# Moving the start addresses of matmul operands in SBUF, and the adaLN sums by one job turn

## The chip, the cores and the metric

The kernel runs on one core of a Trainium2 chip. The metric is the device time of one execution in microseconds (us): the median of three runs is 3477.94 (3477.12 to 3479.91). PE is the matmul engine, PEld its weight loads, DVE, ACT and POOL the three element-wise engines, SP the queue that issues most DMAs.

## The reference

Two transformer-like blocks of two layers each over a sequence of 512 tokens of width 1024, all in float32. What is computed, cut down:

```
first_block, per layer:   ada = silu(c) @ w_ada + b_ada          # adaLN: six vectors of 1024
                          u   = h * (1 + sc1) + sh1
                          y   = mixer(u)    # mLSTM (4 heads), dilated attention (24 heads), gates, w_a, w_b, w_out
                          h   = layer_norm(ALPHA * h + g1 * y)
                          u   = h * (1 + sc2) + sh2
                          h   = layer_norm(ALPHA * h + g2 * ((silu(u @ w1) * (u @ w3)) @ w2))
second_block, per layer:  adaLN, RMS norm, then RG-LRU + stick-breaking attention (layer 0)
                          or windowed attention (layer 1), then a gated FFN with a small convolution
```

Nearly all arithmetic is in products of a 1024- or 2816-wide activation with a weight matrix.

## The kernel before

**Split products.** Activations lie transposed, 128 channels by 512 tokens, in *slots* of 2048 bytes per partition; 60 slots are handed out first in, first out (`get`, `put`). A product needs float32 accuracy, so each operand is split into a high and a low part (`hl`, `split`), and each 128 by 128 weight block costs three matmuls, called a triple here: high x high, low activation x high weight, high activation x low weight. Matmuls of the split type are one pass; each is preceded by the load of its stationary operand (PEld), which runs while the matmul ahead streams.

**Weights.** All 4176 blocks come as one stream: SP loads 16 blocks (1 MB) into `wt`; per *unit* of 8 blocks ACT casts the high part `wh` and DVE subtracts for the low part `wl` (`block`, L589 and L592). Five `wh` and five `wl` tiles rotate, so ACT and DVE run up to 40 blocks ahead of PE.

**Three kinds of split product.** `proj` (L604 to L606; its twins are `begin`, L667 to L669, and the first product, L1367 to L1369) moves a slot's 512 columns over a weight block that stands still: *full* products. `proj_halves` (L649, L652, L653) does the same for 256 columns at a time, at the ends of the layers, where a norm waits: *half* products. `proj_tokens` (L625, L628, L629) lets 256 columns of weights move over 128 columns of a slot: *moving-weight* products. In the mLSTM heads, L961 to L963 multiply two slots in the same three-step way, 512 columns each.

**Where things lie.** The tiles' sizes, in the order in which the pools take them, give every start. Before, each slot begins 448 bytes past a multiple of 512, and each `wh` and `wl` tile 384 bytes past one; a block within a unit is 512 bytes, and half a slot 1024, so all blocks and halves share these. Counted modulo 512, the moving start minus the stationary start is then 64 in full and half products, 448 in moving-weight products, and 0 where slots meet slots (L961 to L963).

**adaLN.** `ada` is a background job. One call of `background()` (a job turn) stands in each pass of the mixer's gate loops and of the FFN loops. A group of 4 x 512 outputs takes four turns, each with four 512 KB loads of `wada` (two buffers) and eight DVE steps into one slot (L776, L778); in the fourth turn, behind the last DVE step, four matmuls sum over partitions (L786), and a last turn transposes and writes columns (L794 on).

**Order.** Queues are in order, and a scheduler places instructions on each engine by what it reckons to be ready; the order below is its outcome. In `attention_pair` each of four query tiles takes, for two heads x, a score slot `p` and a transposed slot `pt`; `bts` are the bias tiles, loaded on POOL's queue (L1115).

Of the kernel before, what the change touches and what calls it, by code (L numbers as in the profile page):

```python
# [10 lines left out]
F32 = mybir.dt.float32  # L11
F32R = mybir.dt.float32r
# [4 lines left out]
P = 128  # L17
# [9 lines left out]
NBLK = 4176  # L27
CHUNK = 16
NCHUNK = NBLK // CHUNK
NSLOT = 60  # L30
NTAIL = 3
NT8 = 5
TT = ['ev_w_out_2']
UNIT = 8
# [161 lines left out]
class Slot:  # L196
# [4 lines left out]
    def __init__(self, i, ap, rounded):  # L201
        self.i = i
        self.r = ap if rounded else None
        self.f = ap.bitcast(F32) if rounded else ap
# [319 lines left out]
class Model:  # L524
    def __init__(self, ctx, tc, ins, out, dbg=None, stop=None):
        self.tc, self.nc, self.ins, self.out, self.dbg_out, self.stop = tc, tc.nc, ins, out, dbg, stop
        self.plan = []
        pool = lambda name, bufs, **kw: ctx.enter_context(tc.tile_pool(name=name, bufs=bufs, **kw))
        self.cp = pool("cp", 1)
        self.wtp = pool("wtp", 2)  # L530
        self.whp = pool("whp", 5)
        self.adp = pool("adp", 2)
        self.drp = pool("drp", 2, space=bass.MemoryType.DRAM)
        self.sm = pool("sm", 4)
        self.pacc = pool("pacc", 3, space=PSUM)
        self.pss = pool("pss", 2, space=PSUM)
        self.pst = pool("pst", 1, space=PSUM)
        self.pso = pool("pso", 2, space=PSUM)
        self.slots = pool("slots", 1)
        self.freeq = deque(range(NSLOT))  # L540
        self.peak = NSLOT
        self.late = []
        self.flip = 0
        self.ready = {}
        self.jobs = deque()
        self.later = []


    def get(self, rounded=False):
# [28 lines left out]
    def block(self, name, l, k, c):  # L578
        nc = self.nc
        n = len(self.plan)  # L580
        self.plan.append((name, l, k, c))
        if n % CHUNK == 0:
            self.wt = self.wtp.tile([P, CHUNK * P], F32, name="wt")
            nc.sync.dma_start(out=self.wt, in_=self.ins["ws"][n // CHUNK].rearrange("p a b -> p (a b)"))
        if n % UNIT == 0:
            self.wh = self.whp.tile([P, UNIT * P], F32R, name="wh")
            self.wl = self.whp.tile([P, UNIT * P], F32R, name="wl")
            src = self.wt[:, (n % CHUNK) * P:(n % CHUNK + UNIT) * P]
            copy = nc.scalar.copy(self.wh, src)  # L589
            if n == 0:  # L590
                self.behind(copy, self.last_rsqrt)
            nc.vector.tensor_tensor(out=self.wl, in0=src, in1=self.wh, op=ALU.subtract)  # L592
        s = slice((n % UNIT) * P, (n % UNIT + 1) * P)
        return self.wh[:, s], self.wl[:, s]
# [14 lines left out]
    def proj_tokens(self, name, l, c, xs):  # L609

        nc = self.nc
        ws = []
        for k in range(len(xs)):
            n = len(self.plan) % UNIT * P
            self.block(name, l, k, c)
            self.block(name, l, k, c + P)
            ws.append((self.wh[:, n:n + 2 * P], self.wl[:, n:n + 2 * P]))
        accs = []
        for a in range(2):
            accs.append(self.pacc.tile([P, T], F32, name="acc"))  # L620
            last = None
            for b in range(2):
                acc, jj = accs[a][:, 256 * b:256 * b + 256], slice((2 * a + b) * P, (2 * a + b + 1) * P)
                for k, (wh, wl) in enumerate(ws):
                    m = nc.tensor.matmul(acc, xs[k].h.r[:, jj], wh, start=k == 0, stop=False)  # L625
                    if k == 0:
                        self.behind(m, last)
                    nc.tensor.matmul(acc, xs[k].l.r[:, jj], wh, start=False, stop=False)  # L628
                    last = nc.tensor.matmul(acc, xs[k].h.r[:, jj], wl, start=False, stop=k == len(xs) - 1)  # L629
        return accs  # L630

    def proj_halves(self, specs, xs, k0=0, by_input=False):


        nc = self.nc
        n = len(xs)
        accs = [self.pacc.tile([P, T], F32, name="acc") if a < 3 else self.pso.tile([P, T], F32, name="o")
                for a in range(len(specs))]
        order = [(a, k) for a in range(len(specs)) for k in range(n)]
        if by_input:  # L640
            order.sort(key=lambda ak: ak[1])
        blks = {}
        last = [None] * len(specs)
        for hs in HALVES:
            for a, k in order:
                if (a, k) not in blks:
                    blks[a, k] = self.block(*specs[a][:2], k0 + k, specs[a][2])
                (wh, wl), acc = blks[a, k], accs[a]
                m = nc.tensor.matmul(acc[:, hs], wh, xs[k].h.r[:, hs], start=k == 0, stop=False)  # L649
                if k == 0:  # L650
                    self.behind(m, last[a])
                nc.tensor.matmul(acc[:, hs], wh, xs[k].l.r[:, hs], start=False, stop=False)  # L652
                last[a] = nc.tensor.matmul(acc[:, hs], wl, xs[k].h.r[:, hs], start=False, stop=k == n - 1)  # L653
                yield hs, a, k == n - 1, acc
# [45 lines left out]
    def setup(self):  # L700
# [3 lines left out]
        n = CST["ident"]  # L704
# [13 lines left out]
        self.zero = zero.to_broadcast([P, T])  # L718
        self.mhalf = self.cp.tile([P, 4], F32, name="mhalf")
        nc.gpsimd.memset(self.mhalf, -0.5)  # L720
        self.ident_r = self.cp.tile([P, 128], F32R, name="ident_r")
        nc.vector.tensor_copy(self.ident_r, self.ident)
        self.csil = self.cp.tile([P, 16], F32, name="csil")
        c = self.vec("c1", 0, 16)
        th = self.small(16, "th_c")
        nc.scalar.activation(th, c, AF.Tanh, scale=0.5)
        nc.vector.tensor_scalar(out=th, in0=th, scalar1=0.5, scalar2=0.5, op0=ALU.mult, op1=ALU.add)
        nc.vector.tensor_mul(self.csil, th, c)
# [20 lines left out]
            for l in range(DEPTH):  # L749
                self.adac[blk, l] = self.cp.tile([P, 48], F32, name=f"ada{blk}{l}")  # L750

        self.vn = [self.cp.tile([P, 4, 258], F32R, name=f"vn{k}") for k in range(2)]
        for k in range(2):
            col = self.small(4, "vcol")
            nc.gpsimd.memset(col, (1 - k) / 16.0)
            for j in (256, 257):
                nc.vector.tensor_copy(self.vn[k][:, :, j], col)


    def ada(self, blk, l, groups):  # L760
        nc = self.nc
        w = self.ins["ada1" if blk == 0 else "ada2"][l]
        bias = f"b_ada{l}" if blk == 0 else f"ada_b{l}"
        ad = self.adac[blk, l]
        for g in groups:
            accs = []
            for n in range(4):
                acc = self.get()
                for q in range(4):
                    wt = self.adp.tile([P, 2, T], F32, name="wada")  # L770
                    nc.sync.dma_start(out=wt, in_=w[4 * g + n, q])
                    for j in range(2):
                        k = 2 * q + j
                        c = self.csil[:, 8 * blk + k:8 * blk + k + 1]
                        if k == 0:
                            nc.vector.tensor_scalar(out=acc.f, in0=wt[:, j, :], scalar1=c, scalar2=None, op0=ALU.mult)  # L776
                        else:
                            nc.vector.scalar_tensor_tensor(out=acc.f, in0=wt[:, j, :], scalar=c, in1=acc.f,  # L778
                                                           op0=ALU.mult, op1=ALU.add)
                accs.append(acc)  # L780
                if n < 3:
                    yield

            rows = self.pss.tile([P, T], F32, name="s")
            for n, acc in enumerate(accs):
# [73 lines left out]

    def load_rsqrt(self, dep):  # L860

        t = self.small(1, "arsd")
        return self.nc.scalar.activation(t, dep, AF.Abs_reciprocal_sqrt, bias=1.0, scale=0.0)


# [179 lines left out]
    def attention_pair(self, l, sp, u):  # L1045
# [62 lines left out]
        o0 = self.pso.tile([P, T], F32, name="o")  # L1108
        o12 = self.pso.tile([P, T], F32, name="o")
        self.lastmm = {}  # L1110
        ls, mx = self.small(16, "att_l"), self.small(16, "att_m")
        cols = lambda ap, x, i: ap.rearrange("p (x y i) -> p x y i", x=2, y=2)[:, x, :, i]
        bts = [self.get(), self.get()]
        for x in range(2):
# [1 line left out]
        for i in (0, 3, 1, 2):  # L1116
            ii = slice(i * P, (i + 1) * P)
            lo, hi = max(0, i * P - 64), min(T, i * P + 192)
            w, u0, at = hi - lo, lo - (i * P - 64), min(lo, T - 256)
# [9 lines left out]
            for x in range(2):  # L1129
# [17 lines left out]
                t = self.pst.tile([P, T], F32, name="t")  # L1147
# [36 lines left out]
        t = self.pst.tile([P, T], F32, name="t")  # L1184
# [5 lines left out]
        w, l0 = self.get(), self.get()  # L1190
# [641 lines left out]
```

## Time and profile before

| | |
|---|---|
| median of three runs | 3477.94 us |
| the profiled execution | 3481.36 us, of which span 3479.6 us |
| PE, PEld busy | 98%, 80% of the span |
| DVE, ACT, POOL busy | 62%, 42%, 5% |
| mean granted TensorE clock | 0.993 |

A matmul's row in the trace is longer than the step from its start to the next start, since neighbours overlap; the pace of PE is read from starts. The difference between the execution and its span, 1.8 us, lies around the span.

### The profile page before, as it was taken

What the parts mean: (1) busy time and instruction counts of PE and PEld (TensorE: products, weight loads), DVE (VectorE), ACT (ScalarE), POOL (GpSimd) and SP (SyncE); (2) the same over time, 40 slices, a digit from 0 to 9 for tenths busy, and PEclk for the clock granted to TensorE, in tenths of its full rate; (3) what the DMA queues carried; (4) which work ended last, traced back from release to release, by engine and by line L of the source; (5) the groups of instructions that cost most, each with busy time, mean ns of one, the idle gap of its engine ahead of it and who ended that gap; (6) DMA issues with size and microseconds to landing.
All of it is one profiled execution on the core that took longest, in us unless ns stands there. A gap on an engine that the chain in (4) does not pass through costs nothing.

```text
span 3479.6 us, 45264 instructions
## 1 busy us (share of the span) xinstructions
PE 3405.2 (98%) x17783; PEld 2787.9 (80%) x17783; DVE 2159.5 (62%) x4071; ACT 1450.8 (42%) x2536; POOL 183.8 (5%) x252
## 2 busy tenths in 40 slices
PE   7999999999999999999999999989999999999999
PEld 5788777778888888877788888877688888888887
DVE  5875545648663687554534856378888555875353
ACT  4543555225222454355523422237753234753231
POOL 1110010010000011001100000001000000000000
PEclk9999999999999999999999999999999999999999
DMA  5222223634552222222222555221146432122222
GB/s 218 91 75 84 75 78 105 223 121 176 205 188 97 73 91 79 80 84 73 79 97 85 200 187 194 94 71 61 37 145 232 163 114 85 50 74 97 97 97 73
DMA packets 76117, 395.72 MB, mean 114 GB/s; under 512 B 9200, under 2 KB 10480, under 8 KB 42496
## 3 DMA queue, kind: packets, MB, share of 16 engines
q1 hardware_dynamic: 69408, 377.90, 30.5%
q0 software_dynamic: 4480, 12.69, 1.2%
q8 instruction: 140, 2.29, 0.3%
q10 hardware_dynamic: 2016, 2.25, 0.2%
q14 instruction: 73, 0.60, 0.1%
HBM read 390.60 MB, written 2.20 MB: 113 GB/s over the span
## 4 chain that ended last, share of the span: by engine, by line
PE 85%; DVE 7%; ACT 2%; DMA 2%; issue 1%; POOL 0%; DVEq 0%; ACTq 0%; POOLq 0%
PE acc L604 22%; PE acc L606 21%; PE acc L605 21%; PE acc L649 2%; PE acc L652 2%; PE acc L653 2%; DMA wada<-in_ada_dram 1%; PE o L1168 1%; PE o L1583 1%; DVE wl L592 1%; PE s L1132 1%; DVE slot L778 1%; PE acc L625 1%; PE acc L629 1%; PE acc L628 1%
## 5 line engine op out<-in xcount | busy, mean ns | idle before, releaser
L604 PE MATMUL acc<-slot,wh 128*128 128x512 f32 x3461 | 1375.7, 398 | 14.0 <-DVE slot L874 9.3
L605 PE MATMUL acc<-slot,wh 128*128 128x512 f32 x3461 | 1364.0, 394 | 0.0
L606 PE MATMUL acc<-slot,wl 128*128 128x512 f32 x3461 | 1363.3, 394 | 0.0
L589 ACT CAST wh<-wt 128x1024 fp32r<-128x1024 f32 x522 | 547.2, 1049 | 1230.0 <-PE acc L605 1021.9
L592 DVE TENSOR_TENSOR wl<-wt,wh 128x1024 fp32r<-128x1024 f32 x522 | 647.7, 1242 | 526.1 <-ACT wh L589 521.3
L604 PEld LDWEIGHTS acc<-slot,wh 128*128 128x128 f32 x3461 | 652.7, 189 | 164.2 <-ACT wh L589 13.9
L606 PEld LDWEIGHTS acc<-slot,wl 128*128 128x128 f32 x3461 | 652.1, 188 | 146.6 <-issue 4.9
L605 PEld LDWEIGHTS acc<-slot,wh 128*128 128x128 f32 x3461 | 652.9, 189 | 140.8 <-issue 5.4
L778 DVE SCALAR_TENSOR_TENSOR slot<-wada,csil,slot 128x512 f32<-128x512 f32 x308 | 232.1, 754 | 63.2 <-DMA wada<-in_ada_dram 57.6
L649 PE MATMUL acc<-slot,wh 128*128 128x256 f32 x726 | 206.9, 287 | 6.2 <-ACT slot L512 5.9
L652 PE MATMUL acc<-slot,wh 128*128 128x256 f32 x726 | 205.6, 283 | 0.0
L653 PE MATMUL acc<-slot,wl 128*128 128x256 f32 x726 | 204.3, 282 | 0.1
L680 ACT CAST slot<-slot 128x512 fp32r<-128x512 f32 x204 | 125.3, 620 | 168.9 <-DVE slot L1332 47.2
L1266 DVE SCALAR_TENSOR_TENSOR slot<-acc,ada,slot 128x512 f32<-128x512 f32 (+1 forms) x109 | 70.2, 647 | 160.8 <-PE acc L606 120.8
L874 DVE SCALAR_TENSOR_TENSOR slot<-acc,vecs,slot 128x510 f32<-128x510 f32 (+2 forms) x217 | 159.9, 746 | 7.8 <-ACT slot L869 5.2
L681 DVE TENSOR_TENSOR slot<-slot,slot 128x512 fp32r<-128x512 f32 x204 | 144.4, 714 | 30.8 <-ACT slot L680 21.3
L649 PEld LDWEIGHTS acc<-slot,wh 128*128 128x128 f32 x726 | 136.8, 189 | 13.4 <-ACT slot L512 6.5
L652 PEld LDWEIGHTS acc<-slot,wh 128*128 128x128 f32 x726 | 137.3, 189 | 2.5 <-issue 1.2
L653 PEld LDWEIGHTS acc<-slot,wl 128*128 128x128 f32 x726 | 137.4, 189 | 0.7 <-DVE wl L592 0.3
L625 PE MATMUL acc<-wh,slot 128*128 128x256 f32 x288 | 81.5, 283 | 0.0
L628 PE MATMUL acc<-wh,slot 128*128 128x256 f32 x288 | 81.4, 283 | 0.0
L629 PE MATMUL acc<-wl,slot 128*128 128x256 f32 x288 | 80.9, 281 | 0.0
(391 smaller groups left out, 3939.6 us busy)
## 6 DMA issues: line engine op xcount, KB each, us to landing
wt<-in_ws_dram SPq DMA_DIRECT2D x261, 1024.0 KB, 4.8
wada<-in_ada_dram SPq DMA_DIRECT2D x176, 512.0 KB, 4.4
slot<-in_ada_dram SPq DMA_DIRECT2D x32, 256.0 KB, 6.1
slot<-drc POOLq DMA_DIRECT2D x16, 256.0 KB, 3.5
slot<-in_bias_dram POOLq DMA_DIRECT2D x16, 256.0 KB, 3.0
slot<-dr POOLq DMA_DIRECT2D x32, 128.0 KB, 3.0
out_dram<-slot SPq DMA_DIRECT2D x8, 256.0 KB, 2.0
slot<-in_xT_dram SPq DMA_DIRECT2D x4, 256.0 KB, 5.4
```

Source lines behind the costliest of these rows:

```text
L589: copy = nc.scalar.copy(self.wh, src)
L592: nc.vector.tensor_tensor(out=self.wl, in0=src, in1=self.wh, op=ALU.subtract)
L604: nc.tensor.matmul(acc, wh, xs[k].h.r, start=k == 0, stop=False)
L605: nc.tensor.matmul(acc, wh, xs[k].l.r, start=False, stop=False)
L606: nc.tensor.matmul(acc, wl, xs[k].h.r, start=False, stop=k == n - 1)
L649: m = nc.tensor.matmul(acc[:, hs], wh, xs[k].h.r[:, hs], start=k == 0, stop=False)
L652: nc.tensor.matmul(acc[:, hs], wh, xs[k].l.r[:, hs], start=False, stop=False)
L653: last[a] = nc.tensor.matmul(acc[:, hs], wl, xs[k].h.r[:, hs], start=False, stop=k == n - 1)
L680: copy = self.nc.scalar.copy(pair.h.r, src)
L681: self.nc.vector.tensor_tensor(out=pair.l.r, in0=src, in1=pair.h.f, op=ALU.subtract)
L778: nc.vector.scalar_tensor_tensor(out=acc.f, in0=wt[:, j, :], scalar=c, in1=acc.f, op0=ALU.mult, op1=ALU.add)
L874: nc.vector.scalar_tensor_tensor(out=out[:, lo:hi], in0=acc[:, lo + d:hi + d], scalar=w, in1=out[:, lo:hi], op0=ALU.mult, op1=ALU.add)
```

## The change

It has three parts. Slots now begin at multiples of 512 bytes: small pads are put between constants, and a few small tiles get fewer buffers. A `wh` or `wl` tile grows by 512 bytes and its unit begins 0 bytes into it (full products), 64 bytes (half products) or 448 bytes (moving-weight products); for the room, the slots go from 60 to 57. With that, moving minus stationary start is 0 in full products, 448 in half and in moving-weight products, and 0 still for slots with slots. Third, the fourth partial sum of adaLN ends a turn of its own, and the four matmuls stand in the next.

```diff
-NSLOT = 60
+NSLOT = 57
+FULL, HALF, MOVING = 0, 16, 112
...
+    def pad(self, pool, n):
+        self.pads += 1
+        t = pool.tile([P, n // 4], F32, name=f"pad{self.pads}", tag=f"pad{self.pads}", bufs=1)
+        self.nc.gpsimd.memset(t[:, 0:1], 0.0)
...
         if n % UNIT == 0:
-            self.wh = self.whp.tile([P, UNIT * P], F32R, name="wh")
-            self.wl = self.whp.tile([P, UNIT * P], F32R, name="wl")
+            at = slice(self.place, self.place + UNIT * P)
+            self.wh, self.wl = (self.whp.tile([P, UNIT * P + P], F32R, name=w)[:, at] for w in ("wh", "wl"))
...
+        self.place = MOVING
         for k in range(len(xs)):
...
+        self.place = FULL
...
                 if (a, k) not in blks:
+                    self.place = HALF
                     blks[a, k] = self.block(*specs[a][:2], k0 + k, specs[a][2])
+                    self.place = FULL
...
-        th = self.small(16, "th_c")
+        th = self.small(16, "th_c", 1)
...
+        self.pad(self.cp, 32)
+        self.pad(self.sm, 64)
...
                 accs.append(acc)
-                if n < 3:
-                    yield
+                yield
...
-        ls, mx = self.small(16, "att_l"), self.small(16, "att_m")
+        ls, mx = self.small(16, "att_l", 2), self.small(16, "att_m", 2)
```

PE's queue at the first adaLN sum, in the mixer of layer 0, before; `s` is the sum's bank, `acc` the bank of the product around it:

```order
L605 MATMUL acc<-slot_5313,wh 128x512
L606 MATMUL acc<-slot_5312,wl 128x512
L786 MATMUL s<-slot_5442,sums 32x512
L786 MATMUL s<-slot_5522,sums 32x512
L786 MATMUL s<-slot_5602,sums 32x512
L604 MATMUL acc<-slot_256,wh 128x512
...
L606 MATMUL acc<-slot_262,wl 128x512
L786 MATMUL s<-slot_5682,sums 32x512
L604 MATMUL acc<-slot_264,wh 128x512
```

And the same place now (the lines are those of the changed file, L807 for L786, L616 to L618 for L604 to L606):

```order
L617 MATMUL acc<-slot_5323,wh 128x512
L618 MATMUL acc<-slot_5322,wl 128x512
L807 MATMUL s<-slot_5452,sums 32x512
L807 MATMUL s<-slot_5532,sums 32x512
L807 MATMUL s<-slot_5612,sums 32x512
L807 MATMUL s<-slot_5692,sums 32x512
L616 MATMUL acc<-slot_266,wh 128x512
```

The four sums stand together, 16 blocks later for the first three and 12 for the fourth. At the group that follows, three and one stay apart, 24 and 22 blocks later than before.

PE's queue near the end of the fourth attention pair of layer 0, before; `o` is the bank of the weighted values, `t` that of a transpose:

```order
L1172 MATMUL o<-slot_5194,slot_5030 64x128
L605 MATMUL acc<-slot_271,wh 128x512
L606 MATMUL acc<-slot_270,wl 128x512
L1150 MATMUL t<-consts,slot_5212 128x128 x2
L1152 MATMUL t<-consts,slot_5212 128x128 x2
L1150 MATMUL t<-consts,slot_5234 128x128 x2
L1152 MATMUL t<-consts,slot_5234 128x128 x2
L1168 MATMUL o<-slot_5224,slot_4796 64x128
```

And now (L1171, L1173 and L1189 are L1150, L1152 and L1168 of before):

```order
L618 MATMUL acc<-slot_272,wl 128x512
L616 MATMUL acc<-slot_274,wh 128x512
L1171 MATMUL t<-consts,slot_5222 128x128 x2
L1173 MATMUL t<-consts,slot_5222 128x128 x2
L617 MATMUL acc<-slot_275,wh 128x512
L618 MATMUL acc<-slot_274,wl 128x512
L616 MATMUL acc<-slot_276,wh 128x512
L617 MATMUL acc<-slot_277,wh 128x512
L1171 MATMUL t<-consts,slot_5244 128x128 x2
L1173 MATMUL t<-consts,slot_5244 128x128 x2
L1189 MATMUL o<-slot_5234,slot_4806 64x128
```

More matmuls of full products stand between the steps of the softmax: from a pair's first score to its end 32, 27, 30 and 24 for the four pairs before, and 34, 37, 48 and 54 now (in layer 1 the last is 57). On POOL's queue the bias loads of the third pair stood ahead of the second pair's `dr` store (L1189 before), and now stand behind its last subtraction (L1199 before).

## Rows read from the trace of the kernel before

**Rows 1.** The page, first part: busy us (share), instructions of each engine.

```profile
PE 3405.2 (98%) x17783; PEld 2787.9 (80%) x17783; DVE 2159.5 (62%) x4071; ACT 1450.8 (42%) x2536; POOL 183.8 (5%) x252
```

**Rows 2.** The page, fourth part: the chain that ended last, by engine.

```profile
PE 85%; DVE 7%; ACT 2%; DMA 2%; issue 1%; POOL 0%; DVEq 0%; ACTq 0%; POOLq 0%
```

**Rows 3.** Groups by line and form, PE: busy, mean ns, idle before.

```profile
L604 PE MATMUL acc<-slot,wh 128*128 128x512 f32 x3461 | 1375.7, 398 | 14.0 <-DVE slot L874 9.3 <-DVE slot L1331 2.7 <-ACT slot L680 1.1
...
L649 PE MATMUL acc<-slot,wh 128*128 128x256 f32 x726 | 206.9, 287 | 6.2 <-ACT slot L512 5.9 <-ACT slot L378 0.3
...
L649 PE MATMUL o<-slot,wh 128*128 128x256 f32 x224 | 63.0, 281 | 0.0
```

**Rows 4.** Timeline of PE, full products in the FFN: start us, us, line.

```profile
2700.11 0.39 PE L604 MATMUL acc<-slot,wh 128*128 128x512 f32 x1
...
2711.78 0.39 PE L604 MATMUL acc<-slot,wh 128*128 128x512 f32 x1
```

**Rows 5.** Stretches: us, busy of PE, PEld, DVE, ACT, POOL, granted clock, DMA.

```profile
2700.00:2750.00 50.00, 50.00 (x220) 41.01 (x219) 20.14 (x23) 9.49 (x9) 0.00 (x0) 1.00 0.33 108
277.70:280.40 2.70, 2.70 (x14) 2.25 (x13) 2.51 (x3) 1.55 (x2) 0.00 (x0) 1.00 0.00 0
355.00:590.00 235.00, 233.49 (x1214) 179.25 (x1214) 120.73 (x376) 121.69 (x281) 22.56 (x48) 1.00 0.22 77
```

**Rows 6.** Timeline of PE in an mLSTM head: slots by slots, then a full product.

```profile
277.69 0.39 PE L961 MATMUL s<-slot,slot 128*128 128x512 f32 x1
...
280.41 0.39 PE L604 MATMUL acc<-slot,wh 128*128 128x512 f32 x1
...
281.79 0.39 PE L961 MATMUL s<-slot,slot 128*128 128x512 f32 x1
```

**Rows 7.** Timeline of PE, half products at two places.

```profile
773.86 0.28 PE L649 MATMUL acc<-slot,wh 128*128 128x256 f32 x1
...
775.98 0.28 PE L649 MATMUL acc<-slot,wh 128*128 128x256 f32 x1
...
789.42 0.28 PE L649 MATMUL acc<-slot,wh 128*128 128x256 f32 x1
...
789.76 0.28 PE L649 MATMUL acc<-slot,wh 128*128 128x256 f32 x1
```

**Rows 8.** Timeline of PE, moving-weight products of the first and second head.

```profile
78.08 0.28 PE L625 MATMUL acc<-wh,slot 128*128 128x256 f32 x1
...
80.80 0.28 PE L625 MATMUL acc<-wh,slot 128*128 128x256 f32 x1
...
148.75 0.28 PE L625 MATMUL acc<-wh,slot 128*128 128x256 f32 x1
...
150.16 0.28 PE L625 MATMUL acc<-wh,slot 128*128 128x256 f32 x1
```

**Rows 9.** Timeline of PE at the first group of adaLN sums.

```profile
641.17 0.40 PE L606 MATMUL acc<-slot,wl 128*128 128x512 f32 x1
...
642.49 0.50 PE L604 MATMUL acc<-slot,wh 128*128 128x512 f32 x1
...
647.06 1.04 PE L786 MATMUL s<-slot,sums 128*32 128x512 f32 x2 [1.54 <-DVE slot L778]
```

**Rows 10.** Timeline of PE at the second group of adaLN sums.

```profile
698.46 1.04 PE L786 MATMUL s<-slot,sums 128*32 128x512 f32 x2 [2.00 <-DVE slot L778]
...
713.58 1.04 PE L786 MATMUL s<-slot,sums 128*32 128x512 f32 x2 [1.73 <-DVE slot L778]
```

**Rows 11.** Timeline of POOL, and of DVE, around the third pair's bias.

```profile
449.59 1.11 POOL L1115 DMA_DIRECT2D slot<-in_bias_dram  x2
...
460.22 1.29 POOL L1199 TENSOR_TENSOR slot<-slot,slot 128x512 f32<-128x512 f32 x1 [4.30 <-DVE slot L1197]
...
494.55 0.36 DVE L1138 CUSTOM_DVE_ANT_0 slot<-s,slot 128x192 f32<-128x192 f32 x1 [2.61 <-PE s L1132]
```

More of the change, by code (lines that the diff above doesn't have):

```diff
@@ L546, in __init__ @@
         self.later = []
+        self.pads = 0
+        self.place = 0
+    def pad(self, pool, n):
+        self.pads += 1
+        t = pool.tile([P, n // 4], F32, name=f"pad{self.pads}", tag=f"pad{self.pads}", bufs=1)
+        self.nc.gpsimd.memset(t[:, 0:1], 0.0)
     def get(self, rounded=False):
@@ L750, in setup @@
                 self.adac[blk, l] = self.cp.tile([P, 48], F32, name=f"ada{blk}{l}")
-        self.vn = [self.cp.tile([P, 4, 258], F32R, name=f"vn{k}") for k in range(2)]
+        self.vn = []
         for k in range(2):
-            col = self.small(4, "vcol")
+            self.pad(self.cp, 32)
+            self.vn.append(self.cp.tile([P, 4, 258], F32R, name=f"vn{k}"))
+        self.pad(self.cp, 32)
+        self.pad(self.sm, 64)
+        for k in range(2):
+            col = self.small(4, "vcol", 1)
             nc.gpsimd.memset(col, (1 - k) / 16.0)
@@ L860, in load_rsqrt @@
     def load_rsqrt(self, dep):
-        t = self.small(1, "arsd")
+        t = self.small(1, "arsd", 1)
         return self.nc.scalar.activation(t, dep, AF.Abs_reciprocal_sqrt, bias=1.0, scale=0.0)
```

## The prediction

> **What bounds the kernel now.** I read the busy times first: PE is busy for 3405.2 us of a span of 3479.6, 98%, and DVE for 62% [rows 1]. The reader is to see that no other engine is near its limit. The chain of waits says the same: 85% of it is PE [rows 2]. Then the groups by line: 3461 full products with three matmuls each, and 726 + 224 = 950 half products; the first line of a full product sat idle for 14.0 us in all [rows 3]. So PE hardly waits, and what counts is the step from one matmul's start to the next, which I take from starts in the timeline. In a quiet stretch of the FFN, 51 matmuls lie between the two rows, in 11.67 us: 228.8 ns a step, 686.5 ns a triple [rows 4]. [...]
>
> **The change part by part.**
>
> *Full products.* Nothing is removed or added; the moving start goes from 64 to 0 bytes past the stationary one, modulo 512. The trace of before has matmuls of the same shape, 128x512, with exactly that relation: the products of slots by slots. Twelve of them take 2.72 us, 226.7 ns each, 680.0 a triple, and the six matmuls of full products right behind them, in the same mLSTM head, take 1.38 us, 230 ns each [rows 6]. Both stretches are at clock 1.00 and PE is busy throughout [rows 5]. So the two relations stand side by side with nothing else changed but where the operands lie. I take the 6.5 ns per triple (686.5 - 680.0): 3461 x 6.5 ns = 22.4 us. It is all on the path, since PE sets the end. The bounds: 0, if the relation is not the cause, and 22.4, as no row shows 512 columns at a lasting pace below 226.7 ns. The twelve rows are in a place where DVE and ACT work as well (2.51 and 1.55 us of 2.70), so I see no reason to take off for company.
>
> [...]
>
> *Half products.* Their relation goes from 64 to 448. With 64 they run 18 matmuls in 2.12 us, 117.8 ns each, at one place, and a triple in 0.34 us, 113.3 each, at another [rows 7]. Moving-weight products, which have 448 already, also show two levels: 24 matmuls in 2.72 us, 113.3 ns, in the first head, and 12 in 1.41 us, 117.5 ns, in the second [rows 8]. So 448 doesn't fix the level; it may make the low one more frequent. The bounds are 0 and 950 x 3 x 4.5 ns = 12.8 us. I take a third, 4.3 us, since neither relation holds one level. Moving-weight products keep their relation: 0.
>
> *The other matmuls.* Transposes, sums and small products, too, read slots that begin elsewhere. PE's busy time less the two kinds above is 3405.2 - 3461 x 0.6865 - 950 x 0.353 = 694 us. If their pace moved by the 1% that parts 680.0 from 686.5, that is 7 us to either side. I take 0, as I know of no sign.
>
> *The adaLN sums.* In the first group three sums stood apart from the fourth. The first three put 642.49 - 641.17 = 1.32 us between two full matmuls, 1.1 us more than a step, and the fourth then waited 1.54 us more for DVE [rows 9]. Now the four stand together, 12 to 16 blocks (8 to 11 us) later, and DVE's last partial sum is only one unit of weights (8 blocks) later in its own queue. That takes away one separate stop and, I think, most of the wait: 1.1 + 1.5 = 2.6 us. In the second group PE waited 2.00 and 1.73 us [rows 10]; there the sums moved 24 and 22 blocks, but DVE's partial sums moved 24 blocks as well, for the loads of `wada` that a turn issues were moved with it. I cost that at nothing. The later groups show no wait to win; one extra turn each fits the loops (18 turns of an FFN for three groups of six, 14 of the mixer for two). Bounds: 0 and 2.6 + 3.7 = 6.3 us. Past SP's queue nothing is moved but the `wada` loads, whose readers wait on DVE, not on PE.
>
> *Three slots fewer.* At the tightest, in the fourth attention pair, 3 of 60 slots were free; now none of 57 is. A score slot is then handed on as soon as its transposes are done, so the next query tile starts later, and the bias loads of the next pair slip behind the last subtraction on POOL's queue. The loads: issued at 449.59 us for a reader at 494.55, they'd now go out at 460.22 + 1.29 = 461.5, 33 us ahead of it [rows 11]; hidden. The softmax: PE fills the gaps with full products, 18 and 30 more in the third and fourth pairs. PE was busy for 233.49 of the 235 us of this stage [rows 5], and these products are work taken from later, not added; I cost it at 0. If that cover is gone, and the pairs grow by as much as was put in while the places left empty stay empty, it is 2 layers x 48 x 0.229 us = 22 us. A gain is bounded by the 1.5 us that PE is not busy there, twice: 3 us.
>
> *The sum.* 22.4 + 4.3 + 2.6 = 29.3 us off the profiled execution's 3481.36 gives 3452.1. The median of the runs lies 3.4 us below that execution, so I put the median at 3448.6, in round figures 3448.
>
> **The rivals.**
>
> *A: starts don't matter.* The pace stays at 686.5 ns a triple, and the slots by slots are fast for another reason, such as that their stationary operand was not just written by ACT and DVE. For it: half products show two levels with one relation [rows 7], so something besides the starts chooses. Against it: rows 6. Only the sums are left: 3477.94 - 2.6 = 3475. [...]
>
> *B: the missing slots take the gain back.* The pace falls, but the attention pairs stretch, and PE waits. For it: no slot is free at the tightest place. Against it: the products that are put between. With the full 22 us the time is 3470; with half, 3459.
>
> *C: a worse pace, so slower than before.* Moving operand, `wh` and `wl` of full products now all begin at multiples of 512. The two levels of half and moving-weight products, 113.3 and 117.8 ns, are 4% apart [rows 7, 8]. If full products fell into such an upper level, a triple would take 680 x 1.04 = 707 ns, 20.5 more than now: 3461 x 20.5 ns = 71 us, about 3542 with the 2.6 of the sums. It decides from a triple of some 690.5 ns on: 4 ns more on 3461 triples is 13.8 us, which eats the smaller gains and the bound of no change. Against it: no lasting run of full products or of slots by slots is above 230 ns in rows 4 and 6.
>
> **How the numbers follow.** My forecast has 0.72; A 0.09; B 0.13; C 0.06. The forecast's own range runs from 3429 (22.4, 12.8, 6.3 and 7 us all gained) to 3462 (half of the gain in pace, no other). The range of 3429 to 3471 takes in B and the forecast and leaves out A and C, 0.15, and a little at the low end. A run of this kernel can be told from no change from about 0.2% on, 7 us. Faster by more than that is the forecast and nearly all of B, 0.83; within it, A and the end of B, 0.10; slower, C and a small rest, 0.07.
>
> **What would show it.** In the changed profile, 17 blocks of a full product in the quiet FFN should take 11.56 us instead of 11.67, and slots by slots stay at 2.72 us for twelve; if both are at 228.8, A holds, and above 230, C. Half products should show 113.3 ns at more places than now. The first group of sums should be one row of eight with no wait for DVE behind it, the second still split with waits near 2 us. The fourth attention pair should be longer, with PE's idle time before its rows no larger. A pace below 226.7 ns would mean that a start counts by itself, not only the relation, and the time would leave the range at the low end.

## The result, and the profile after

The changed kernel takes **3496.64 us** (median of 4 runs, 3494.85 to 3499.55) against 3477.53 of the kernel before: ratio 1.0055, interval 1.0037 to 1.0072. In a second set of runs, in which the experiments below were timed too, it came to 3496.84 against 3480.85: 1.0042 (1.0027 to 1.0057). So it is slower by 15 to 19 us, where I had forecast 30 us off. The profiled execution took 3499.55 us, its span is 3497.8.

The busy times are first, the page's first part, as in [rows 1]:

```profile
PE 3398.8 (97%) x17783; PEld 2791.3 (80%) x17783; DVE 2158.0 (62%) x4071; ACT 1454.3 (42%) x2536; POOL 186.1 (5%) x257
```

PE is busy for 6.4 us less than in [rows 1], yet the span is 18.2 us longer. So PE worked faster and stood still for longer. Both halves can be read. First the pace, in PE's timeline of the same stretches as [rows 4, 6, 7] (a product's first line was L604 and is L616, L649 is L665, L961 is L982):

```profile
2722.06 0.39 PE L616 MATMUL acc<-slot,wh 128*128 128x512 f32 x1
...
2733.62 0.39 PE L616 MATMUL acc<-slot,wh 128*128 128x512 f32 x1
...
275.86 0.39 PE L982 MATMUL s<-slot,slot 128*128 128x512 f32 x1
...
278.58 0.39 PE L616 MATMUL acc<-slot,wh 128*128 128x512 f32 x1
...
279.94 0.39 PE L982 MATMUL s<-slot,slot 128*128 128x512 f32 x1
...
782.22 0.28 PE L665 MATMUL acc<-slot,wh 128*128 128x256 f32 x1
...
784.34 0.28 PE L665 MATMUL acc<-slot,wh 128*128 128x256 f32 x1
...
2349.88 0.28 PE L665 MATMUL acc<-slot,wh 128*128 128x256 f32 x1
...
2352.60 0.28 PE L665 MATMUL acc<-slot,wh 128*128 128x256 f32 x1
```

Seventeen blocks take 11.56 us, as forecast (11.67 in [rows 4]). Twelve products of slots by slots still take 2.72 us, and the six matmuls of full products behind them now have the same step, 1.36 us against 1.38 in [rows 6]. Half products still have two levels: 18 in 2.12 us (117.8 ns) at one place, 24 in 2.72 (113.3) at another. Over all their triples the low level now holds for 64% instead of 17% (52% in a second profile of the same kernel, `e0_after`).

Then the standing still. The first line of the full products, in the groups by line (busy us, mean ns, then PE's idle time before it and who ended it), to be held against the first of [rows 3]:

```profile
L616 PE MATMUL acc<-slot,wh 128*128 128x512 f32 x3461 | 1368.5, 395 | 31.1 <-ACT slot L1249 14.3 <-DVE slot L895 10.7 <-DVE slot L1352 4.4
```

The idle time is 31.1 us instead of 14.0, and a releaser stands first that [rows 3] does not have: 14.3 us for ACT's L1249. That is the tanh in the mixer's gate loop (L1228 before), which empties an `acc` bank into the tile `th`. PE's timeline shows the larger of its two waits, at the end of layer 0's attention, and what follows it:

```profile
601.63 0.39 PE L618 MATMUL acc<-slot,wl 128*128 128x512 f32 x1
610.72 0.79 PE L616 MATMUL acc<-slot,wh 128*128 128x512 f32 x1 [8.71 <-ACT slot L1249]
...
612.17 0.63 PE L616 MATMUL acc<-slot,wh 128*128 128x512 f32 x1
612.59 0.63 PE L617 MATMUL acc<-slot,wh 128*128 128x512 f32 x1
...
615.58 0.45 PE L618 MATMUL acc<-slot,wl 128*128 128x512 f32 x1
...
1749.27 0.80 PE L616 MATMUL acc<-slot,wh 128*128 128x512 f32 x1 [5.57 <-ACT slot L1249]
```

PE stops for 8.71 us, and when it goes on its first step is 0.59 us and those behind it 0.42 to 0.43 us, instead of 0.23. Layer 1 has the same stop. The stretches (us, busy of PE, PEld, DVE, ACT, POOL, granted clock, DMA) show the attention pairs of layer 0, as in [rows 5], then the first stop, the second, and a third place, the end of the stick-breaking attention:

```profile
352.00:598.00 246.00, 243.39 (x1264) 186.13 (x1262) 125.93 (x382) 126.22 (x287) 22.68 (x48) 1.00 0.21 75
605.40:615.70 10.30, 4.98 (x12) 3.92 (x13) 5.57 (x8) 2.99 (x4) 1.26 (x1) 0.50 0.19 55
1738.70:1752.30 13.60, 8.03 (x21) 6.12 (x22) 5.20 (x7) 4.04 (x5) 3.39 (x6) 0.75 0.31 117
2519.00:2549.00 30.00, 23.05 (x104) 16.13 (x105) 18.29 (x35) 20.05 (x48) 0.00 (x0) 0.72 0.00 0
```

In the pairs themselves PE is as busy as before, 243.39 of 246 us. At the first stop the granted clock is 0.50; PE had been idle from 602 on, and the 11 steps from 610.72 to 615.58 take 4.86 us. So this stop is paid twice. In the third place PE is busy for 23.05 of 30 us, at a mean clock of 0.72. In the kernel before, this is the least busy of the eight 10 us stretches from 2470 to 2550 us, where that stage ends:

```profile
2500.00:2510.00 10.00, 8.79 (x53) 5.77 (x51) 9.05 (x20) 7.31 (x21) 1.36 (x2) 1.00 0.01 2
```

The fourth attention pair did grow, as forecast: it takes 33.2 us (563.2 to 596.4) from its first score to its last weighted value, instead of 26.4 (564.3 to 590.7).

Why ACT was late is seen in its own timeline, and in DVE's:

```profile
608.26 1.28 ACT L1219 ACT_TABLE_LOAD   x1 [5.39 <-DVE slot L1218]
609.55 0.63 ACT L1219 ACTIVATE slot<-slot 128x512 f32<-128x512 f32 x1
610.09 0.58 ACT L1249 ACTIVATE slot<-acc 128x512 f32<-128x512 f32 x1
...
607.17 1.02 DVE L1218 TENSOR_TENSOR slot<-slot,slot 128x512 f32<-128x512 f32 x1 [3.04 <-DMA slot<-dr]
```

The gate's tanh (L1249) has had its input since 602 at the latest, when PE's last product was done, but stands in ACT's queue behind the tanh of `d` (L1219), which waits for the subtraction `w - l0` (L1218), which waits for a DMA through DRAM. In the kernel before, the same two rows of ACT stand the other way round (L1228 is the gate, L1198 the tanh of `d`):

```profile
593.53 0.60 ACT L1228 ACTIVATE slot<-acc 128x512 f32<-128x512 f32 x1
...
602.73 0.63 ACT L1198 ACTIVATE slot<-slot 128x512 f32<-128x512 f32 x1 [3.34 <-DVE slot L1197]
```

The order follows from the slots. Slots are handed out first in, first out, and 57 come round three `get`s sooner than 60. With 60 the first `th` gets a slot that held keys of the fourth pair, long read; with 57 it gets the one of `l0`, which that DMA fills and L1218 reads. So the gate's tanh can't be put ahead of L1218 any more. Most of its delay is this wait for the slot: L1218 has read it only at 608.19, wherever the tanh stands in ACT's queue. The rest, to 610.09, is its place behind the table load and the tanh of `d`.

Last the adaLN sums, to be held against [rows 9, 10]:

```profile
662.20 1.96 PE L807 MATMUL s<-slot,sums 128*32 128x512 f32 x8
...
719.23 1.05 PE L807 MATMUL s<-slot,sums 128*32 128x512 f32 x4
720.47 1.05 PE L807 MATMUL s<-slot,sums 128*32 128x512 f32 x2 [0.19 <-DVE slot L800]
...
734.66 1.47 PE L807 MATMUL s<-slot,sums 128*32 128x512 f32 x2 [2.71 <-DVE slot L800]
```

The first group is one row of eight without a wait, the second is still split with a wait of 2.71 us: both as forecast. Here too the clock falls behind the wait: it is 0.50 from 735.2 to 738.5 us, and two sums take 1.47 us instead of 1.05.

### The profile page after: what moved, and what is told of

It reads as the page before. It is cut to its first block, busy times and chain, and to the rows that moved or that the text cites. A ratio compares the mean times of both kernels' runs of the same rounds, so it can differ in the third digit from the quotient of the medians.

```text
span 3497.8 us, 45346 instructions
## 1 busy us (share of the span) xinstructions
PE 3398.8 (97%) x17783; PEld 2791.3 (80%) x17783; DVE 2158.0 (62%) x4071; ACT 1454.3 (42%) x2536; POOL 186.1 (5%) x257
## 4 chain that ended last, share of the span: by engine, by line
PE 44%; DVE 4%; ACT 1%; issue 1%; DMA 0%; DVEq 0%; ACTq 0%
PE acc L616 12%; PE acc L618 12%; PE acc L617 11%; PE acc L665 1%; PE acc L669 1%; PE acc L668 1%; PE o L1604 1%; PE t L1707 0%; DVE wl L604 0%; PE s L1487 0%; DVE slot L1584 0%; PE o L665 0%; PE o L668 0%; PE o L669 0%; PE s L1488 0%
## 5 line engine op out<-in xcount | busy, mean ns | idle before, releaser
L616 PE MATMUL acc<-slot,wh 128*128 128x512 f32 x3461 | 1368.5, 395 | 31.1 <-ACT slot L1249 14.3
L618 PE MATMUL acc<-slot,wl 128*128 128x512 f32 x3461 | 1359.1, 393 | 0.0
L604 DVE TENSOR_TENSOR wl<-wt,wh 128x1024 fp32r<-128x1024 f32 x522 | 645.5, 1238 | 512.3 <-ACT wh L601 504.0
L616 PEld LDWEIGHTS acc<-slot,wh 128*128 128x128 f32 x3461 | 654.1, 189 | 179.5 <-ACT slot L1249 15.1
L618 PEld LDWEIGHTS acc<-slot,wl 128*128 128x128 f32 x3461 | 653.3, 189 | 136.8 <-issue 5.0
L665 PE MATMUL acc<-slot,wh 128*128 128x256 f32 x726 | 206.9, 287 | 6.8 <-ACT slot L515 6.0
L665 PEld LDWEIGHTS acc<-slot,wh 128*128 128x128 f32 x726 | 137.9, 191 | 14.2 <-ACT slot L515 6.6
L1159 DVE CUSTOM_DVE_ANT_0 slot<-s,slot 128x256 f32<-128x256 f32 (+1 forms) x128 | 48.2, 402 | 56.9 <-PE o L1193 31.4
```

The costliest lines, as they stand in the source:

```text
L616: nc.tensor.matmul(acc, wh, xs[k].h.r, start=k == 0, stop=False)
L618: nc.tensor.matmul(acc, wl, xs[k].h.r, start=False, stop=k == n - 1)
```

## The experiments

Theory S: the missing slots cost the time, by the order on ACT at the end of the attention and by a like effect in the stick-breaking attention, while starts and sums gain. The rivals put the stops down to the new starts, to the pads, or to the later sums. All ratios below are to the kernel before on the same chip, from 5 to 11 runs each (one for the sweep).

**57 slots and nothing else** (`e1_slots57`)

```diff
-NSLOT = 60
+NSLOT = 57
```

> The kernel before with 57 slots instead of 60 and nothing else changed. Theory S (the three missing slots cost the time: the gate loop's first tanh stands behind the last tanh of the attention and PE stops for 8.9 and 5.7 us, and the stick-breaking attention runs out of products): slower by what the changed kernel lost and, in addition, by what its pace gained, 19 + 20 = 39 us, so about 3515 us (3500 to 3525), with a stop of 5 us or more at about 600 and 1740 us of the profile. Rival R (the new starts, the pads or the turn of the adaLN sums bring the stops): 3477 within 7 us, and no such stops.

Measured: 3511.59 us, 1.0095 (1.0079 to 1.0111), 33 us more by the ratio (31 by the medians). PE's waits, the longest in total first (us in total, times, longest):

```profile
PE acc L604 <- ACT slot L1228: 15.4, 2, 9.0
PE acc L604 <- DVE slot L874: 8.2, 3, 3.7
```

The new wait heads the list, with the old starts and the old sums, and the third place is there too:

```profile
2530.00:2540.00 10.00, 7.20 (x25) 4.61 (x26) 3.90 (x11) 6.91 (x18) 0.00 (x0) 0.64 0.00 1
2540.00:2550.00 10.00, 7.37 (x28) 5.55 (x27) 9.58 (x13) 7.69 (x17) 0.00 (x0) 0.67 0.00 0
```

The number of slots alone makes them. S holds; R is out.

**60 slots, everything at multiples of 512** (`e2_starts60`)

```diff
-NSLOT = 57
-FULL, HALF, MOVING = 0, 16, 112
+NSLOT = 60
+FULL, HALF, MOVING = 0, 0, 0
...
-            self.wh, self.wl = (self.whp.tile([P, UNIT * P + P], F32R, name=w)[:, at] for w in ("wh", "wl"))
+            self.wh, self.wl = (self.whp.tile([P, UNIT * P], F32R, name=w)[:, at] for w in ("wh", "wl"))
```

> The changed kernel with all 60 slots: slots, wt, wada, wh and wl all begin at multiples of 512, the units of weights have no longer tile and no offset (half and moving-weight products then have relation 0 instead of 448), the adaLN sums come one turn later. Theory S: the stops are gone and the pace stays, so faster than the kernel before by 20 to 25 us: 3455 (3448 to 3464); a full triple at 680 ns. Rival R: the stops stay at about 600, 1740 and 2520 to 2548 us, and the time is 3485 or more.

Measured: 3467.71 us, 0.9958 (0.9945 to 0.9972), -13 us. The stops are gone, a full triple takes 681 ns. But it misses 3455 and its range: half and moving-weight triples rose to 360 ns (351 and 347 before). For 256 columns relation 0 is the slower one here.

**The late hand-back** (`e3_lateput`)

```diff
-        self.put(l0, w, d, o12s)
+        self.over = (l0, w, d, o12s)
+        if sp < 3:
+            self.put(*self.over)
         return o0s
...
             hmp.append(pr)
+        self.put(*self.over)
         ya = []
```

> The changed kernel, but the fourth attention pair's last four slots (l0, w, d, o12s) are handed back only after the loop that splits hm, so that the gate loop's first tanh takes a slot that has long been free. Theory S: the stops of 8.9 and 5.7 us and the half clock behind them (10.2 and 6.8 us at half speed, so some 8 us) go: 3496.6 - 22 = 3475 (3470 to 3485). Rival: the stop is not due to the order on ACT but to acc banks being full anyway, and moves to the next product: 3496 within 5 us.

Measured: 3474.77 us, 0.9987 (0.9979 to 0.9996), 22 us under the changed kernel (19 by the ratios), as expected. The same 30 us in the changed kernel and in this one:

```profile
590.00:620.00 30.00, 20.68 (x92) 15.44 (x91) 15.41 (x30) 11.74 (x20) 3.83 (x6) 0.83 0.29 94
```

```profile
590.00:620.00 30.00, 29.61 (x140) 22.91 (x140) 23.79 (x38) 13.45 (x20) 3.88 (x6) 1.00 0.62 207
```

PE is busy for 29.61 us instead of 20.68, and the clock stays at 1.00. The gate's tanh (L1252 here) stands ahead of the tanh of `d` again:

```profile
598.61 0.60 ACT L1252 ACTIVATE slot<-acc 128x512 f32<-128x512 f32 x1
...
611.26 0.63 ACT L1219 ACTIVATE slot<-slot 128x512 f32<-128x512 f32 x1 [2.29 <-DVE slot L1218]
```

This changes no start (modulo 512), no sum and no number of slots, only when four slots come back and so which slot `th` and the tiles behind it get. So the slot that `th` takes is the cause of that stop. The run does not part the wait for that slot from the place in ACT's queue that comes with it.

**The later sums alone** (`e4_ada`)

```diff
                 accs.append(acc)
-                if n < 3:
-                    yield
+                yield
```

> The kernel before with the adaLN sums one turn later and nothing else changed. My prediction: 2.6 us faster (0 to 6.3), so 3475. Theory S: within 4 us of the kernel before. Rival R' (the later sums add waits, as the 2.9 and 0.9 us at 731 and 735 us of the changed kernel's profile would suggest): slower by 4 to 10 us.

Measured: 3474.80 us, 0.9982 (0.9972 to 0.9991), -6 us (3 to 10 by the interval), the upper bound of my term and 2 us more than theory S allowed. PE's waits before the sums fall from 5.3 us in all to 0.9. R' is out.

**All of the change with 60 slots** (`e5_offsets60`)

```diff
-            self.wh, self.wl = (self.whp.tile([P, UNIT * P + P], F32R, name=w)[:, at] for w in ("wh", "wl"))
+            wp = self.whp.tile([P, 2 * UNIT * P + P], F32R, name="wp")
+            self.wh, self.wl = wp[:, at], wp[:, self.place + UNIT * P:self.place + 2 * UNIT * P]
...
+                        wt = self.adp.tile([P, T], F32, name="wada")
+                        nc.sync.dma_start(out=wt, in_=w[4 * g + n, q][:, j, :])
```

> All that the change does, and 60 slots: wh and wl lie in one longer tile (five tiles of 8704 bytes instead of ten of 4608), wada comes in halves of one block each (three tiles instead of two double ones), att_lt has one buffer; half products at relation 448, moving-weight products at 448, full products at 0. Against the 60-slot kernel whose units all begin at 0, half products should go from 360 to about 345 ns a triple (950 x 15 = 14 us) and moving-weight products from 360 to about 350 (288 x 10 = 3 us). Theory S (pace and slots account for everything): 17 us below that kernel, which is 30 below the kernel before: ratio 0.9915 (0.990 to 0.994). Rival (the half products' pace is hidden behind other waits): no faster than the 60-slot kernel, 0.996.

Measured: 3459.55 us, 0.9942 (0.9926 to 0.9958), -21 us. Faster than both kernels, but 8 us (6 by the ratios) and not 17 under `e2_starts60`, just outside the range: half triples fell to 349 ns only (a third of them at the low level), moving-weight ones to 352.

**The changed kernel again** (`e0_after`)

> The changed kernel once more, beside the others on the same chip, as their common point. Ratio to the kernel before 1.0055 as first measured (1.004 to 1.007).

Measured: 3496.84 us, 1.0042 (1.0027 to 1.0057).

**The changed kernel with the old turn of the sums** (`e6_oldsums57`): `e4_ada`'s edit taken back.

> The changed kernel with the adaLN sums at their old turn: new starts and 57 slots only. At 60 slots the later sums gained 6 us. If they gain as much with 57 slots, this kernel is 6 us slower than the changed one (ratio 1.007). If 57 slots turn the gain into a loss (the accumulators of a group then stay in their slots one turn longer, and the waits at 731 and 735 us come from it), it is 5 to 15 us faster than the changed one (0.998 to 1.004).

Measured: 3496.40 us, 1.0047 (1.0031 to 1.0064), the same as the changed kernel. Neither guess is met: with 57 slots the later sums are worth 0 to 2 us, uncertain by some 8, with 60 they were worth 6. By time alone the two are not clearly apart. PE's waits before the sums point the same way: 3.7 us in all here and 4.2 in `e0_after`, where 60 slots went from 5.3 to 0.9.

**All relations in one run** (`e7_sweep`), on `e5_offsets60`:

```diff
+            self.place = 16 * (n // UNIT % 8)
             at = slice(self.place, self.place + UNIT * P)
```

> The 60-slot kernel with offsets, but unit number u of the weights begins 64 x (u mod 8) bytes into its tile, whatever the kind of product. The trace then holds each kind of product at all eight relations in one run. Theory S (only the relation of moving and stationary start modulo 512 sets the pace): full triples 680 ns at offset 0 and 687 at offset 448 (relation 64), half triples 360 at offset 0, 352 or 340 at 448, 340 or 352 at 64; the others unknown. Rival (the pace comes from what else runs, not from starts): the eight groups differ by less than 2 ns.

PE's timeline in the quiet FFN, the first matmul of nine units in a row; a unit is 24 matmuls, its relation goes 448, 384, 320, ... 0, 448:

```profile
2702.34 0.40 PE L618 MATMUL acc<-slot,wp 128*128 128x512 f32 x1
...
2707.94 0.39 PE L618 MATMUL acc<-slot,wp 128*128 128x512 f32 x1
...
2713.51 0.39 PE L618 MATMUL acc<-slot,wp 128*128 128x512 f32 x1
...
2719.02 0.39 PE L618 MATMUL acc<-slot,wp 128*128 128x512 f32 x1
...
2724.47 0.40 PE L618 MATMUL acc<-slot,wp 128*128 128x512 f32 x1
...
2730.07 0.39 PE L618 MATMUL acc<-slot,wp 128*128 128x512 f32 x1
...
2735.64 0.39 PE L618 MATMUL acc<-slot,wp 128*128 128x512 f32 x1
...
2741.16 0.39 PE L618 MATMUL acc<-slot,wp 128*128 128x512 f32 x1
...
2746.61 0.40 PE L618 MATMUL acc<-slot,wp 128*128 128x512 f32 x1
```

The units take 5.60, 5.57, 5.51, 5.45, 5.60, 5.57, 5.52, 5.45 us, so the pattern comes again after four: it has a period of 256 bytes. Over all undisturbed steps of the run (below 245 and 131 ns; mean ns of some 580 to 2600 steps each):

| moving minus stationary start, modulo 256 | 0 | 64 | 128 | 192 |
|---|---|---|---|---|
| 512 columns (full) | 227.5 | 229.7 | 232.3 | 233.2 |
| 256 columns (half) | 119.8 | 117.8 | 118.5 | 115.3 |

One kernel, one run, nothing differs but the starts of the weights: they set the pace of full products, and the best for 512 columns is the worst for 256. That the difference of the two starts counts, and not the weights' start by itself, rests on two other runs: in the kernel before the starts are 448 and 384 modulo 512, in `e10_oldstarts57` (below) 0 and 448, the difference is 64 in both, and a triple takes 686.9 and 687.0 ns. The one time, 3495.97 us, is 36 us above `e5_offsets60`, whose own runs spread over 9 us. A mean step of 230.7 instead of 227 gives 3461 x 3 x 3.7 ns = 38 us, so here nearly all of the pace seems to have been on the path. Rival A would give no difference; the units' 5.45 to 5.60 us disagree.

**Late hand-back, and `u` handed back early in the stick-breaking attention** (`e8_late_early`), on `e3_lateput`:

```diff
                         following = heads(pr + 1)
+                        if pr == 2:
+                            self.put(u)
...
-        self.put(u, self.strict)
+        self.put(self.strict)
```

> The changed kernel (57 slots) with the late hand-back of the fourth attention pair's slots and, in the stick-breaking attention, the 16 slots of u handed back after the last projection that reads u (as the third of four head pairs begins its second query tile) instead of at the end. Theory S (with 57 slots the last head pair takes slots that the pair before has only just left, so its softmax runs one behind the other and PE runs out of products at 2515 to 2550 us): the stops there go, 8 us below the kernel with the late hand-back alone, ratio to before 0.9987 - 0.0023 = 0.9964 (0.995 to 0.9975). Rival (the stretch is short of products whatever the slots): as the late hand-back alone, 0.9987.

Measured: 3463.30 us, 0.9948 (0.9932 to 0.9963), 12 us under `e3_lateput` (14 by the ratios), which still had the third place. The stretches of `e3_lateput`, then of this one:

```profile
2490.00:2500.00 10.00, 7.34 (x45) 4.45 (x43) 6.69 (x15) 5.88 (x17) 0.00 (x0) 1.00 0.00 0
2500.00:2510.00 10.00, 7.95 (x25) 5.78 (x26) 5.67 (x12) 8.64 (x19) 0.00 (x0) 0.66 0.00 1
2510.00:2520.00 10.00, 7.31 (x37) 5.33 (x35) 6.76 (x11) 5.80 (x13) 0.00 (x0) 0.66 0.00 0
```

```profile
2490.00:2500.00 10.00, 9.79 (x57) 6.90 (x56) 9.21 (x20) 8.97 (x27) 0.00 (x0) 1.00 0.01 2
2500.00:2510.00 10.00, 9.32 (x49) 6.38 (x50) 7.89 (x15) 8.79 (x19) 0.00 (x0) 1.00 0.00 0
2510.00:2520.00 10.00, 9.82 (x68) 6.65 (x66) 9.49 (x21) 6.95 (x22) 0.00 (x0) 1.00 0.01 2
```

PE is busy for 28.9 of 30 us instead of 22.6, and the clock stays at 1.00 there. With both hand-backs 57 slots are as fast as 60, within the intervals.

**The same at 60 slots** (`e9_best`: `e5_offsets60` with the early hand-back; `e11_control60`: with the late one as well)

> The 60-slot kernel with offsets, with the same early hand-back of u. Theory S: at 60 slots 3 were still free at this place, so the gain is small: 0 to 5 us below the 60-slot kernel with offsets, ratio 0.9935 (0.992 to 0.9945).

> The control for the two hand-backs: the 60-slot kernel with offsets and the early hand-back of u, now with the late hand-back of the fourth pair's slots as well. At 57 slots the late hand-back was worth 19 us and both together 33. Theory S (they repair what 57 slots broke, and nothing else): no change at 60 slots, ratio to before 0.9937 (0.992 to 0.9955). Rival (they are improvements of their own): 0.988 to 0.991.

Measured: 3460.10 us, 0.9937 (0.9919 to 0.9954), and 3459.33 us, 0.9936 (0.9923 to 0.9949). Neither differs from `e5_offsets60`: the hand-backs mend what 57 slots broke and gain nothing of their own.

**The old relations with 57 slots** (`e10_oldstarts57`)

```diff
-FULL, HALF, MOVING = 0, 16, 112
+FULL, HALF, MOVING = 112, 112, 112
```

> The changed kernel with all weight units begun 448 bytes into their tiles: full and half products are back at relation 64 and moving-weight products at 448, as before the change; 57 slots and the later sums stay. Theory S (the starts gave what my first term says, and the slots took more): slower than the changed kernel by 3461 x 6 ns + 950 x 5 ns = 25.5 us, ratio to before 1.0042 + 0.0073 = 1.0115 (1.009 to 1.014). Rival (starts don't matter to the time, PE's stalls take up the difference): 1.004 to 1.006.

Measured: 3513.16 us, 1.0091 (1.0075 to 1.0108): 17 us above the changed kernel by the ratios (16 by the medians), uncertain by some 8. The starts are worth something in time, so the rival is out; whether it is less than the 25.5 of their pace, the times alone don't decide.

## Why the prediction was wrong

**The step that failed: "Three slots fewer ... I cost it at 0", with 22 us as its upper bound.** It measured 33 us alone (`e1_slots57`) and 35 with the rest of the change (1.0042 against 0.9942, the weights laid out otherwise). I looked at the tightest place, the fourth attention pair, and there the cover held as I said: PE is busy for 243.4 of 246 us. The cost lay behind it. A first-in-first-out list of slots also decides which old reader a new tile has to wait for, and with it the order in ACT's queue; the stop that follows comes when the products that were pulled ahead have filled the three `acc` banks and PE has nothing else to run. The two hand-backs give 22 and 12 us (19 and 14 by ratio), which is the whole cost. The bound failed for two reasons: it took the lost time to be at most the length of the pulled products, and it knew nothing of the granted clock, which was 0.50 from 610.72 to 615.58, from 1749.27 to 1752.30 and from 2529 to 2534 us, so at each of the three places. The third place was in a stage that the prediction did not look at.

**Full products: the size was right in pace, less sure in time.** 5.9 ns per triple (mean of undisturbed triples 686.9 and 681.0) instead of 6.5, so 20.4 us of pace. Half products gained 6 us (351.1 to 344.9 ns; 4 us in `e0_after`, 346.5 ns; I had 4.3). Moving-weight ones lost 1.6 us (346.5 to 352; I had 0), but not by their starts: `e10_oldstarts57` has the same starts for them and takes 346.1. In all that is 23 to 25 us of pace. By the ratios the starts gave 17 us at 57 slots (`e10_oldstarts57`), 17 again with the old sums (`e1_slots57` to `e6_oldsums57`), and 14 at 60 (`e4_ada` to `e5_offsets60`, with another layout of the weights). Each of these differences is uncertain by some 8 us. "It is all on the path" was probably too much: in one profile of each, from `e10_oldstarts57` to `e0_after`, the steps that begin with a full product's matmul sum up to 11.6 us less and not 20.4, so some 9 us came back as waits or slower steps among them. The other matmuls, which I put at 0, gained nothing there: all three kinds of product together save 18.0 us, the span 16.1.

**The sums.** The forms of both groups were forecast, the worth was not: 6 us at 60 slots (I had 2.6, at most 6.3), and 0 to 2 at 57, where the waits before them stay. Why they stay is open.

**The rivals.** A is out (`e7_sweep`). B named the right part of the change, but at most 22 us of it, and in the pairs. C's mechanism does exist, for 256 columns: at relation 0 half products slowed from 351 to 360 ns (`e2_starts60`). Full products did not at 0, but they too have a slow relation, 192, with 233.2 ns a step or some 700 a triple (`e7_sweep`). Two of the prediction's sums are off: C's 71 us less the 2.6 of the sums give 3546, not 3542, and half of the forecast gain in pace, 13.4 us, with nothing else ends the forecast's own range near 3465, not 3462. Neither changes the outcome.

**Still open.** What chooses between the two levels of half and moving-weight products at one relation (113.3 and 117.5 ns); a level lasts for dozens of products, and moving-weight products with the very same starts had the low one in a tenth of their triples in `e0_after` and in half of them in `e10_oldstarts57`. And which slot's reader made the softmax of the stick-breaking attention run one behind the other; that more free slots cure it is shown, the reader was not followed.

## What to carry to other kernels

A tile taken from a first-in-first-out list inherits the last reader of its memory. When buffers are cut, follow the first tiles handed out behind the tightest place and see on whose late reader they now wait, on engines that empty PSUM above all; handing those buffers back a little later, or others a little earlier, can be worth as much as the buffers. And a change of alignment that is paid for with buffers is to be timed with and without the loss of buffers: here the version that keeps all 60 slots (`e5_offsets60`) beats both kernels, at 0.9942.

## What the runs showed of the hardware

- In `e7_sweep` the mean step of back-to-back float32r matmuls went with the moving minus the stationary start modulo 256 bytes. At 512 columns 0 had the shortest, 227.5 ns, and 192 the longest, 233.2 ns, 2.5% more; at 256 columns 0 had the longest, 119.8 ns, and 192 the shortest, 115.3 ns. Only multiples of 64 bytes were tried.
- The stop of 8.71 us in the changed kernel cost 2.4 us more behind it, at a granted clock of 0.50: the 11 steps from 610.72 to 615.58 took 4.86 us, and would take 2.50 at 227 ns.
